# Last sample sequence of a hybrid decoder step: sliding weights turned ahead of the older values, tokens asked for together, first gate tile's tanh ahead of the next tile's splits

## The chip, the cores and the metric

The kernel runs on one core of a Trainium2 chip. A core has TensorE (PE, matrix products and transposes by a product with the identity), VectorE (DVE), ScalarE (ACT), GpSimd (POOL) and SyncE (SP); the last two issue most of the transfers here. Each engine works through its own instructions in order. The metric is the device time of one execution in microseconds, as a median of runs. All of the arithmetic is in 32-bit floats; a factor of a large product is split into a high and a low part, and three of the four partial products are taken.

## What is computed

One layer of a decoder step, on a prompt of 512 tokens and on 8 sample sequences of 8 new tokens with 2048 cached tokens each. Two attention branches (one with forgetting gates, one with compressed, selected and sliding-window keys) go through a projection each, are merged by sigmoid gates, and are followed by an output projection and an MLP. What matters for the change, cut from the reference:

```python
g_fox, g_nsa = jnp.split(jax.nn.sigmoid(mg), 2, axis=-1)     # mg: columns of h @ w_in
...
s = jnp.einsum('btgrd,bwgd->bgrtw', q, kw) * scale - m * dw   # sliding window of a sample sequence
p_w = masked_softmax(s, (dw >= 0) & (dw < WINDOW) & (w_pos >= 0)[None, :])
o_w = jnp.einsum('bgrtw,bwgd->btgrd', p_w, vw)
...
br_fox = jnp.einsum('btk,kd->btd', o_fox.reshape(b, t_len, FOX_QW), lp['w_br_fox'])
br_nsa = jnp.einsum('btk,kd->btd', o_nsa.reshape(b, t_len, NSA_QW), lp['w_br_nsa'])
mix = pm['g_fox'] * br_fox + pm['g_nsa'] * br_nsa
```

The gates need the normalized tokens h of all 576 rows (512 prompt, 64 sample), which earlier in the kernel were written to device memory (`hfd`), turned so that channels lie on the partitions: 8 pieces of 128 channels x 576 tokens.

## The kernel before, in words

The step is a chain of stages: projections, the prompt's attention, the sample sequences' attention (`sample_attention`, L1613, about 430 to 545 us), the mix (`mix_part`, L1967, about 545 to 698 us), the output projection and the MLP.

**The order.** The program is written in one order, and a planner sorts each engine's instructions by its own estimate of when they are ready. Where that isn't wanted the code pins it: `chain` and `link` (L87) string all of PE's instructions one behind another as written, from the sample attention's start to its end and again from the second gate tile on. `issue_after(x)` queues what its block writes on x's engine behind x; instructions of other engines in the block aren't held by it. `dma` (L151) keeps the order of transfers on one queue.

**The sample loop** (L1651). For each of the 8 sequences b: scores (`sequence_scores`, PE, then four reductions on DVE), scores of the new tokens (`new_scores`), the maximum and three exponentials on ACT (`sequence_max`), turns of the weights on PE with copies on ACT (`turn_weights`, into `T` and `TN`), and the products with the values (`values`, into the bank `so`). The sliding window is done for two sequences at a time, n = b // 2: its weights `SWt` are made in the even sequence and turned in the odd one (`window_turned`, L1907: four turns into bank `spw` and one of the new tokens into `spwn`, then two ACT copies to `TW` and `TWn`), then multiplied by the values (`window_values`) and summed by `pair_sums` one pair later. For the last sequence, b = 7, sequence 6's older values (its parts 2 and 3) are written between the scores and `new_scores`, by a function given to `sequence_scores`. The trace names `TW` and `SWt` both `scr`.

**The tokens.** At b = 7 the buffers of sequence 6 are free and become `hL` and `hH`, the low and high parts of h. `tokens_load` (L1602) first writes a few elements of `hL` on ACT from a source that is a gate (so that the loads wait for it) and then asks for the pieces on SP and POOL by turns: pieces 0 to 3 after the new scores, with `CT` as the gate; pieces 4 to 7 in `turn_weights`, with `TN`. Each piece is split: ACT makes `hH`, DVE makes `hL` (L1727 to L1733, four ahead of the last values and four behind). `mix_first` (L1958) takes the products of the high parts for the first gate tile.

**The mix.** For each of 8 tiles of 128 output channels there are two gates (tanh of half the product h w) and two branch products; `branch` multiplies, `closed` adds and splits the sum. Weights come through one ring of three raw buffers (`praw`): a load goes into a buffer, ACT and DVE split it (`stream`, L170), then the buffer is free for the next load. Tile 0 and 1 take their gates as plain products; tiles 2 to 7 take both gates as one 2 x 2 block product with seven multiplications (`pair`, L2079), whose token operands `token_sums` (L2012) makes from the rows of h. For that the rows are loaded again: `rows_ahead` (L2002) writes one element on ACT behind the last high part, and then POOL asks for `hr0` (pieces 0 to 2), `mgtr` (pieces 3 and 7) and `hr1` (pieces 4 to 6). There are four PSUM banks for products (`mmb`); a gate's bank is free when its tanh on ACT has read it, a branch's when DVE has multiplied it.

Of the kernel before, what the change touches and what calls it, by code (L numbers as in the profile page):

```python
# [6 lines left out]
F32 = mybir.dt.float32  # L7
# [3 lines left out]
AF = mybir.ActivationFunctionType  # L11
# [3 lines left out]
P = 128  # L15
D = 1024
NK = D // P
SEQ = 512
NB = 8
NS = 64  # L20
NT = SEQ + NS
HALF = NT // 2
TOK = 2080
# [22 lines left out]
class Step:  # L46
# [1566 lines left out]
    def sample_attention(self, sp, ctx):  # L1613
# [35 lines left out]
        last = NB - 1  # L1649

        for b in range(NB):  # L1651
            n, odd = b // 2, b % 2
            if b and b + 2 < NB:
                self.key_prep(b + 2)
            self.sequence_scores(b, (lambda: self.values(b - 1, range(2, 4))) if b == last else None)
            ahead = not odd and b > 2
            if ahead:
                for o in range(2):
                    self.window_keys(b + o)
            self.new_scores(b)  # L1660
            if not odd:
                self.window_new(n)
            if not odd and b:
                self.values(b - 1, range(1, 4))
            if b == last:
                self.hL = self.keep.tile([P, 5 * D], F32R, tag="r2", bufs=1, name="hL2")[:, 0:NK * NT].rearrange("p (k t) -> p k t", k=NK)
                self.hH = self.rp.tile([P, NK, NT], F32R, tag="rp", name="hH")
                self.tokens_load(range(4), self.CT[0:1, 0:4, None])
            self.sequence_max(b)
            if odd:  # L1670
                self.window_turned(n)
            if b > 1:
                self.sequence_end(b - 2)
                if not odd:
                    self.window_end(n - 1)
            if b < last:
                with self.tc.issue_after(self.last_stat):
                    self.key_turn(b + 1, (0, 1))
            if 0 < b < last and odd:
                self.values(b - 1, range(2, 4))  # L1680
            if b == last - 1:
                self.mix_ahead()
            if odd:
                self.window_values(n)
                if b < last:
                    for o in range(2):
                        self.window_load(b + 1 + o, "gpsimd")
                if b > 1:
                    self.pair_sums(n - 1)
            if b and b + 2 < NB:  # L1690
                self.sample_load(b + 2, range(1 if b % 2 == 0 else 2, 4))
            if b < last:
                with self.tc.issue_after(self.last_stat), self.tc.issue_after(self.last_end) if b > 1 else nullcontext():
                    self.key_counts(b + 1)
                    self.key_turn(b + 1, (2, 3))
            if b == last:
                self.sequence_end(b - 1)
                self.window_end(n)
                ctx.close()
                self.mix_open()  # L1700
                with self.tc.issue_after(self.last_exp):
                    self.w0 = self.gate_weights(0, 0)
            if b == 0:
                for o in range(2):
                    self.window_keys(o)
            if ahead:
                self.window_scores(n)
            self.turn_weights(b)
            if b == 2:
                with self.tc.issue_after(self.last_weights):  # L1710
                    for o in range(2):
                        self.window_keys(b + o)
            if b < last:
                with self.tc.issue_after(self.last_weights):
                    self.last_weights = self.act(self.CT, self.ct).ins
            if b < last:
                self.values(b, range(1 if odd else 2))
            if b + 3 < NB:
                self.sample_load(b + 3, range(1 if odd else 2))
            if not odd:  # L1720
                if not ahead:
                    self.window_scores(n)
                self.window_weights(n)
            if b == 0:
                with self.tc.issue_after(self.last_stat):
                    self.sample_maps(maps)
        with self.tc.issue_after(self.last_weights):  # L1727
            for k in range(4):
                self.split(self.hH[:, k], self.hL[:, k], self.hL[:, k].bitcast(F32))
        self.values(last, range(4))  # L1730
        with self.tc.issue_after(self.last_weights):
            for k in range(4, NK):
# [107 lines left out]
    def turn_weights(self, b):  # L1840

        last = b == NB - 1
        tb = self.trb(f"spn{b}")
        self.tr(tb[:NS, 0:P], self.SN[b % 2])
        self.act(self.TN, tb[:NS, 0:P])
        if last:
            self.tokens_load(range(4, NK), self.TN[0:1, 0:NK - 4, None])
        for i in range(4):
            tb = (self.trb if last and i > 1 else self.mmb)(f"sp{b}{i}")
            for j in range(4):  # L1850
                self.tr(tb[:, P * j:P * j + P], self.S[:, 4 * i + j].rearrange("p q s -> p (q s)"))
            self.last_weights = self.act(self.T[i], tb.rearrange("p (j n) -> p j n", j=4)).ins
# [52 lines left out]
            self.act(self.SWt, self.SWt, AF.Exp, bias=st[:, 2:3], accum_out=st[:, 3:4])  # L1905

    def window_turned(self, i):  # L1907
        tb, tn = self.trb(f"spw{i}"), self.mmb(f"spwn{i}")
        for j in range(4):
            self.tr(tb[:, P * j:P * j + P], self.SWt[:, P * j:P * j + P])  # L1910
        self.tr(tn[:NS, 0:P], self.SWt[:, 512:576])
        self.act(self.TW, tb.rearrange("p (j n) -> p j n", j=4))
        self.act(self.TWn, tn[:NS, 0:P])

    def window_values(self, i):
        col = 256 + 128 * (i % 2)
# [15 lines left out]
        self.mctx = ExitStack()  # L1932
        self.pqr = self.pool("pqr", self.mctx, side="right")

    def gate_weights(self, e, x):
        return self.stream(self.pqr, self.cols(self.I["w_in"], TOK + D * x + P * e, P), [P, NK, P], "wm", f"{x}_{e}", raws=0, parts=1)

    def mix_ahead(self):

# [27 lines left out]
    def mix_part(self, pq, pr, mix2):  # L1967
# [16 lines left out]
            return pq.tile([P, 2, 2, HALF], F32, tag="c", bufs=2, name=f"mgt{e}")  # L1984

        def gate(out, pb):
            self.act(out, pb, AF.Tanh, scale=0.5)

        def branch(e, x, w, C):
            pbs = [half(f"br{e}{x}", w, (hs(oH, 4 * x), hs(oL, 4 * x)), 4, hf) for hf in range(2)]  # L1990
# [4 lines left out]
        def br_weights(e, x):  # L1995
            return self.stream(pq, self.br_src(x, e), [P, 4, P], "wb", f"{x}_{e}", raws=0, parts=1)
# [3 lines left out]
            self.split_pack(mix2[:, e], C[:, 0].rearrange("p g t -> p (g t)"))  # L2000

        def rows_ahead(C):  # L2002
            R = [self.pw0.tile([P, 4, 512], F32, tag="w0", bufs=2, name=f"hr{j}").rearrange("p a c -> p (a c)")[:, 0:3 * NT]
                 .rearrange("p (k t) -> p k t", k=3) for j in range(2)]
            R3 = C.rearrange("p f g t -> p (f g t)").rearrange("p (j k t) -> p j k t", j=2, k=1)
            with self.tc.issue_after(self.last_weights):
                self.act(R[0][0:1, 0, 0:1], hH[0:1, NK - 1, 0:1].bitcast(F32))
            for r, k in ((R[0], slice(0, 3)), (R3[:, :, 0], slice(3, 8, 4)), (R[1], slice(4, 7))):
                self.dma("gpsimd", r, self.hfd[:, k])
            return [(slice(0, 3), R), (slice(3, 4), [R3[:, j] for j in range(2)])]  # L2010

        def token_sums(rows):  # L2012
            t12 = self.keep.tile([P, 5 * D], F32R, tag="r1", bufs=1, name="mt12")[:, 0:16 * HALF].rearrange(
                "p (a k t) -> p a k t", a=4, k=4)
            t4 = pq.tile([P, 2, 4, HALF], F32R, name="mt4")
            T = [(t12[:, 0], t12[:, 1]), (t12[:, 2], t12[:, 3]), (b[0][1][0], b[0][1][1]), (t4[:, 0], t4[:, 1])]
            cut = [slice(0, HALF), slice(HALF, NT)]
            for ks, R in rows:
                (r11, r12), (r21, r22) = [[r[:, :, c] for c in cut] for r in R]

                def keep(t, x):
                    self.split(t[0][:, ks], t[1][:, ks], x)

                self.tt(r11, r12, r11, sub)
                keep(T[0], r11)
                self.tt(r12, r22, r12, sub)
                self.tt(r22, r22, r11, sub)
                keep(T[1], r22)
                self.tt(r21, r21, r22, sub)
                keep(T[3], r21)  # L2030

            def last():
                for ks, R in rows:
                    self.split(T[2][0][:, ks], T[2][1][:, ks], R[0][:, :, cut[1]])

            return T, last
# [83 lines left out]
        for x in range(2):  # L2120
# [8 lines left out]
                            self.mm(p, w[:, k, :], h(k, hf), k == 0 and c == 0, k == NK - 1 and c == 2)  # L2129
            for hf in range(2):  # L2130
                gate(C[:, x, hf], pbs[hf][:, 0:HALF])
        for x in range(2):
            branch(0, x, ws[x][1], C)
        closed(0, C)

        ws = [(self.gate_weights(1, x), br_weights(1, x)) for x in range(2)]
        T, last = token_sums(rows)
        C = cs(1)
        self.chain = ""
        for hf in (1, 0):  # L2140
# [566 lines left out]
```

## Time and profile before

| what | value |
|---|---|
| median of 3 runs | 1157.57 us (1155.44 to 1160.59) |
| the profiled execution's own time | 1160.21 us |
| its span | 1158.5 us |
| busy PE, DVE, ACT, POOL | 1093.5, 822.5, 544.4, 243.1 us |
| PE's share of the chain that ended last | 74% |
| moved by the transfers | 191.75 MB, mean 166 GB/s |

A line of the groups or of the order of time has a line number of the code (often that of a helper: L77 is every product, L83 every turn, L112 every ACT operation, L131 the low half of every split, L155 a transfer), the engine, the operation, and output<-inputs by the program's names without numbers. In the order of time the first number is the start in the span and the second the time it covers; `x4` says that four are merged, and a bracket gives the idle time of the engine before it and what ended it. SPq is SP's queue of transfers. PE is pipelined, so its instructions overlap.

### The profile page before, as it was taken

To read this page: it belongs to the slowest core of one execution; us is meant where nothing else is said; L and a number is where in the kernel's file an instruction comes from. 1 tells how busy PE (TensorE), PEld (TensorE's weight loads), DVE (VectorE), ACT (ScalarE), POOL (GpSimd) and SP (SyncE) were. 2 spreads that over 40 slices of the span, in tenths; PEclk is the share of its full clock that TensorE was granted. 3 is DMA by queue.
4 is the path that set the end of the run, shared out by engine and by line. 5 is a ranking of instruction groups with operands and counts; after the bars stand their busy time and mean duration, and the time that the engine had idled before them with its cause. 6 is when DMAs were issued, how large, how long until landed. Compare 5 with 4: busy or idle time off the path is not lost.

```text
span 1158.5 us, 24596 instructions
## 1 busy us (share of the span) xinstructions
PE 1093.5 (94%) x9089; PEld 941.1 (81%) x9089; DVE 822.5 (71%) x2011; ACT 544.4 (47%) x1146; POOL 243.1 (21%) x341
## 2 busy tenths in 40 slices
PE   3999999989999997887999999999999999999998
PEld 3887799989666654556999999998989989898896
DVE  5898666685787857776878667759757567475668
ACT  3466643444777754456545434473424324143230
POOL 7541000001211536440000000013222122221202
PEclk9999999999999998998999999999999999999999
DMA  8998584764786589995632454152313224132232
GB/s 202 296 268 219 200 267 148 254 204 134 248 272 202 146 264 356 361 329 138 183 86 79 110 178 140 47 174 90 110 37 109 73 74 130 52 110 62 66 119 82
DMA packets 167513, 191.75 MB, mean 166 GB/s; under 512 B 17849, under 2 KB 145282, under 8 KB 165218
## 3 DMA queue, kind: packets, MB, share of 16 engines
q1 hardware_dynamic: 151650, 146.80, 42.8%
q0 software_dynamic: 13568, 42.34, 11.2%
q8 instruction: 71, 1.16, 0.4%
q10 hardware_dynamic: 2176, 1.05, 0.4%
q14 instruction: 48, 0.39, 0.1%
HBM read 179.89 MB, written 31.16 MB: 182 GB/s over the span
## 4 chain that ended last, share of the span: by engine, by line
PE 74%; DVE 9%; DMA 7%; ACT 4%; issue 3%; POOL 1%; SPq 1%; POOLq 1%; DVEq 0%; ACTq 0%
PE dn L77 18%; PE hid L77 6%; PE z L77 5%; PE wo L77 4%; PE up L77 4%; PE upx L77 3%; PE upv L77 3%; PE br L77 3%; PE ss L77 3%; DMA winr<-in_w_in 3%; PE upy L77 2%; PE upz L77 2%; PE upu L77 2%; PE mgv L77 2%; PE ada L77 1%
## 5 line engine op out<-in xcount | busy, mean ns | idle before, releaser
L100 DVE TENSOR_TENSOR acc<-acc,dn 128x512 f32<-128x512 f32 x66 | 44.5, 685 | 55.4 <-PE dn L77 55.4
L77 PE MATMUL hid<-xh,w1hlk 128*128 128x256 f32 (+1 forms) x192 | 47.4, 340 | 16.5 <-ACT xh L112 16.5
L77 PE MATMUL z<-winh,h2r 128*128 128x264 f32 (+1 forms) x288 | 57.7, 290 | 4.0 <-ACT adw L112 4.0
L77 PE MATMUL z<-winh,h 128*128 128x264 f32 (+1 forms) x288 | 56.8, 287 | 0.0
L112 ACT ACTIVATE xh<-cpg 128x512 fp32r<-128x512 f32 x64 | 37.6, 623 | 36.3 <-PE hid L77 22.5
L112 ACT ACTIVATE u<-c 128x512 fp32r<-128x512 f32 x64 | 24.1, 434 | 58.9 <-PE dn L77 45.1
L77 PE MATMUL hid<-xh,w1hlv 128*128 128x256 f32 (+1 forms) x192 | 47.9, 341 | 4.0 <-ACT w1hlv L112 2.5
L2374 POOL TENSOR_TENSOR wur<-wur 128x512 f32<-128x512 f32 x12 | 19.9, 1658 | 150.3 <-DVE wu1l L131 54.9
L131 DVE TENSOR_TENSOR xl<-cpg,xh 128x512 fp32r<-128x512 f32 x64 | 42.4, 683 | 11.5 <-ACT xh L112 11.5
L77 PEld LDWEIGHTS z<-winh,h2r 128*128 128x128 f32 x288 | 45.8, 190 | 5.3 <-ACT adw L112 4.2
L77 PEld LDWEIGHTS hid<-xh,w1hlk 128*128 128x128 f32 x192 | 33.1, 201 | 20.4 <-ACT xh L112 16.7
L77 PEld LDWEIGHTS z<-winh,h 128*128 128x128 f32 x288 | 46.6, 193 | 0.0
L77 PE MATMUL z<-winl,h 128*128 128x264 f32 (+1 forms) x160 | 44.9, 287 | 0.5 <-DVE winl L131 0.5
L77 PE MATMUL z<-winl,h2r 128*128 128x264 f32 (+1 forms) x160 | 44.7, 286 | 0.0
L470 DVE STREAM_TRANSPOSE cpg<-cpg 128x1024 f32<-128x1024 f32 (+1 forms) x36 | 39.1, 1108 | 6.9 <-DMA cpg<-in_cache_nsa_kv 6.9
L155 POOL DMA_DIRECT2D cpg<-in_cache_nsa_kv x72 | 37.9, 527 | 28.4 <-issue 13.2
L155 POOL DMA_DIRECT2D sr<-in_cache_nsa_kv x64 | 34.6, 542 | 35.1 <-DMA fr<-foxD 10.1
L77 PE MATMUL br<-oH,wbh 128*128 128x288 f32 x128 | 38.4, 300 | 2.6 <-ACT mgt L112 2.6
L77 PEld LDWEIGHTS hid<-xh,w1hlv 128*128 128x128 f32 x192 | 33.6, 202 | 8.2 <-ACT w1hlv L112 2.7
L77 PE MATMUL br<-oL,wbh 128*128 128x288 f32 x128 | 38.4, 300 | 0.0
L77 PE MATMUL br<-oH,wbl 128*128 128x288 f32 x128 | 38.4, 300 | 0.0
L1805 DVE CUSTOM_DVE_ANT_1 sS<-ss,scr 128x512 f32<-128x512 f32 x32 | 20.2, 687 | 22.1 <-PE ss L77 22.1
(887 smaller groups left out, 3628.4 us busy)
## 6 DMA issues: line engine op xcount, KB each, us to landing
adw<-in_w_ada SPq DMA_DIRECT2D x16, 1024.0 KB
foxD<-in_cache_fox_kv SPq DMA_DIRECT2D x128, 128.0 KB
wur<-in_w_up SPq DMA_DIRECT2D x32, 512.0 KB
wdr<-in_w_down SPq DMA_DIRECT2D x32, 512.0 KB
wada<-in_w_ada SPq DMA_DIRECT2D x8, 1024.0 KB
sr<-in_cache_nsa_kv SPq DMA_DIRECT2D x64, 128.0 KB
fr<-foxD SPq DMA_DIRECT2D x16, 512.0 KB
fr<-foxD POOLq DMA_DIRECT2D x16, 512.0 KB, 7.9
```

What stands on the lines that cost most here:

```text
L77: ins = self.nc.tensor.matmul(out, a, b, start=start, stop=stop, skip_group_check=True)
L100: self.nc.vector.tensor_tensor(out, a, b, op=op)
L112: return self.nc.scalar.activation(out, in_, f, **kw)
L131: self.splits.append((eng or self.nc.vector).tensor_tensor(l, x, h.bitcast(F32), op=OP.subtract).ins)
L155: self.issued[eng] = getattr(self.nc, eng).dma_start(out, in_).ins
L470: self.flipped = self.nc.vector.transpose(v, v).ins
L1805: self.nc.vector.tensor_tensor_reduce(self.S[:, :, q, :], pbs[q].rearrange("p (c s) -> p c s", s=32), self.ramp[:, None, 32 * (q % 2):32 * ...
L2374: gp(a12, a12, a11, op=OP.subtract)
```

## The change

In the last sequence, `window_turned` (the four turns into `spw` and the copy to `TW`) is written ahead of sequence 6's older values, directly behind the scores. The turn of the new tokens into `spwn` and the copy to `TWn` become `window_turned_new`, written ahead of the exponentials. For the other odd sequences both follow each other where they were, and the `TW` copy stands ahead of the `spwn` turn. The loads of the token pieces 4 to 7 take `TWn` as their gate in place of `TN`. The two larger row loads (`hr0`, `hr1`) are asked for behind the fourth high part; the third (`mgtr`) stays in `rows_ahead`, now with no gate of its own. The ACT halves of the splits of the second tile's gate weights, and of the token sums up to the last two, are queued behind the first tile's last tanh.

```diff
-            self.sequence_scores(b, (lambda: self.values(b - 1, range(2, 4))) if b == last else None)
+            self.sequence_scores(b, self.last_between if b == last else None)
...
+            if b == last:
+                self.window_turned_new(n)
             self.sequence_max(b)
-            if odd:
+            if odd and b < last:
                 self.window_turned(n)
+                self.window_turned_new(n)
...
+        self.rows_again = [self.pw0.tile([P, 4, 512], F32, tag="w0", bufs=2, name=f"hr{j}").rearrange("p a c -> p (a c)")
+                           [:, 0:3 * NT].rearrange("p (k t) -> p k t", k=3) for j in range(2)]
+        with self.tc.issue_after(self.last_high):
+            self.last_weights = self.act(self.rows_again[0][0:1, 0, 0:1], self.hH[0:1, 3, 0:1].bitcast(F32)).ins
+        for j in range(2):
+            self.dma("gpsimd", self.rows_again[j], self.hfd[:, 4 * j:4 * j + 3])
         self.values(last, range(4))
...
-        if last:
-            self.tokens_load(range(4, NK), self.TN[0:1, 0:NK - 4, None])
...
     def window_turned(self, i):
-        tb, tn = self.trb(f"spw{i}"), self.mmb(f"spwn{i}")
+        tb = self.trb(f"spw{i}")
         for j in range(4):
             self.tr(tb[:, P * j:P * j + P], self.SWt[:, P * j:P * j + P])
+        self.act(self.TW, tb.rearrange("p (j n) -> p j n", j=4))
+
+    def window_turned_new(self, i):
+        tn = self.mmb(f"spwn{i}")
         self.tr(tn[:NS, 0:P], self.SWt[:, 512:576])
-        self.act(self.TW, tb.rearrange("p (j n) -> p j n", j=4))
         self.act(self.TWn, tn[:NS, 0:P])
+        if i == NB // 2 - 1:
+            self.tokens_load(range(4, NK), self.TWn[0:1, 0:NK - 4, None])
+
+    def last_between(self):
+        self.window_turned(NB // 2 - 1)
+        self.values(NB - 2, range(2, 4))
...
-    def gate_weights(self, e, x):
-        return self.stream(self.pqr, self.cols(self.I["w_in"], TOK + D * x + P * e, P), [P, NK, P], "wm", f"{x}_{e}", raws=0, parts=1)
+    def gate_weights(self, e, x, first=None):
+        return self.stream(self.pqr, self.cols(self.I["w_in"], TOK + D * x + P * e, P), [P, NK, P], "wm", f"{x}_{e}", raws=0, parts=1,
+                           pin=first and (first,))
...
-            self.act(out, pb, AF.Tanh, scale=0.5)
+            self.last_gate = self.act(out, pb, AF.Tanh, scale=0.5).ins
...
-            for r, k in ((R[0], slice(0, 3)), (R3[:, :, 0], slice(3, 8, 4)), (R[1], slice(4, 7))):
-                self.dma("gpsimd", r, self.hfd[:, k])
+            self.dma("gpsimd", R3[:, :, 0], self.hfd[:, 3:8:4])
...
                 def keep(t, x):
-                    self.split(t[0][:, ks], t[1][:, ks], x)
+                    with self.tc.issue_after(first):
+                        self.split(t[0][:, ks], t[1][:, ks], x)
...
+        first = self.last_gate
         for x in range(2):
             branch(0, x, ws[x][1], C)
         closed(0, C)
 
-        ws = [(self.gate_weights(1, x), br_weights(1, x)) for x in range(2)]
-        T, last = token_sums(rows)
+        ws = [(self.gate_weights(1, x, first), br_weights(1, x)) for x in range(2)]
+        T, last = token_sums(rows, first)
```

More of the change, by code (lines that the diff above doesn't have):

```diff
@@ L2002, in rows_ahead, with token_sums @@
         def rows_ahead(C):
-            R = [self.pw0.tile([P, 4, 512], F32, tag="w0", bufs=2, name=f"hr{j}").rearrange("p a c -> p (a c)")[:, 0:3 * NT]
-                 .rearrange("p (k t) -> p k t", k=3) for j in range(2)]
+            R = self.rows_again
             R3 = C.rearrange("p f g t -> p (f g t)").rearrange("p (j k t) -> p j k t", j=2, k=1)
-            with self.tc.issue_after(self.last_weights):
-                self.act(R[0][0:1, 0, 0:1], hH[0:1, NK - 1, 0:1].bitcast(F32))
-            for r, k in ((R[0], slice(0, 3)), (R3[:, :, 0], slice(3, 8, 4)), (R[1], slice(4, 7))):
-                self.dma("gpsimd", r, self.hfd[:, k])
+            self.dma("gpsimd", R3[:, :, 0], self.hfd[:, 3:8:4])
             return [(slice(0, 3), R), (slice(3, 4), [R3[:, j] for j in range(2)])]
-        def token_sums(rows):
+        def token_sums(rows, first):
             t12 = self.keep.tile([P, 5 * D], F32R, tag="r1", bufs=1, name="mt12")[:, 0:16 * HALF].rearrange(
```

## The prediction

> **What bounds the kernel now.** I read the page first. It says that TensorE carries most of the chain that ended last, so I asked where TensorE does not run densely near the edits. That is the view of the stages.
>
> ```profile
> span 1158.5 us, 24596 instructions
> ...
> 601.30:700.00 98.70, 98.53 (x742) 98.02 (x741) 69.72 (x131) 41.54 (x73) 2.64 (x5) 1.00 0.45 128
> 700.00:766.00 66.00, 65.04 (x541) 64.40 (x541) 44.71 (x139) 30.94 (x63) 2.77 (x5) 1.00 0.35 110
> 766.00:1158.50 392.50, 387.54 (x2236) 345.93 (x2234) 267.47 (x401) 136.82 (x253) 88.97 (x60) 1.00 0.29 88
> ```
>
> Columns: stretch, length, then busy time of PE, PE's weight loads, DVE, ACT and POOL, the granted clock, DMA share, GB/s. From 601.3 us on PE is busy for nearly all of each stretch, at full clock. A start earlier there by some microseconds therefore moves the end by as much. What decides is when PE reaches 601.3, so next I read the chain of waits from the last sample sequence to there (start, length, what).
>
> ```profile
> 534.10 2.26 ACT sS L112 x4
> 536.36 0.49 ACT scr L112
> ...
> 536.89 1.82 PE so L77 x48
> 538.72 1.05 PE accS L77 x16
> 539.77 0.35 PE spn L83
> ...
> 541.01 0.61 ACT spT L112
> ...
> 542.24 6.11 DMA hL<-hfd
> ...
> 549.77 0.75 DVE hL L131
> ...
> 551.19 1.14 DVE wml L131
> ...
> 552.34 11.04 DMA wmr<-in_w_in
> ...
> 570.38 1.22 DVE wml L131
> ...
> 572.23 7.15 DMA wgr<-in_w_in
> ...
> 589.31 6.70 DMA wgr<-in_w_in
> ...
> 599.44 1.85 PE mgv L77 x12
> ```
>
> Two things run through it. Up to 541 it is a queue: the copy of the turned sliding weights (`scr`, 536.36) stands behind the last sequence's exponentials on ACT, and PE's sliding values, sums and turns stand behind that copy. From 551 on it is the ring of three raw weight buffers: a split frees a buffer (551.19), the next load takes 11.04 us, and so on to `mgv` at 599.44. PE itself shows two gaps, in the order of time of its instructions and ACT's (the bracket is the idle time and what ended it):
>
> ```profile
> 528.71 0.19 ACT L112 ACTIVATION_READ_ACCUMULATOR scr<-scr,swst 128x1 f32 x1
> 531.76 0.66 PE L83 MATMUL spw<-identF,scr 128*128 128x128 f32 x4
> 532.25 0.27 PE L83 MATMUL spwn<-identF,scr 128*64 128x128 f32 x1
> 545.16 0.40 PE L77 MATMUL mg<-hH,wmh 128*128 128x288 f32 x1
> 558.70 0.29 PE L77 MATMUL mg<-hL,wmh 128*128 128x288 f32 x1
> 563.41 1.06 ACT L112 ACTIVATE wmh<-wmr 128x1024 fp32r<-128x1024 f32 x1 [6.51 <-DMA wmr<-in_w_in]
> 564.37 0.69 ACT L112 ACTIVATE mgt<-mg 128x288 f32<-128x288 f32 x2
> 564.82 0.40 PE L77 MATMUL br<-oH,wbh 128*128 128x288 f32 x1 [2.65 <-ACT mgt L112]
> 569.53 0.39 PE L77 MATMUL mg<-hH,wmh 128*128 128x288 f32 x1
> ```
>
> The first gap goes from 532.52 (end of `spwn`) to 536.89, 4.37 us. The second is the 2.65 us before 564.82: a tanh (`mgt`) waits on ACT behind a split (`wmh`) whose weights are still on the way. The granted clock (last but two) fell around both:
>
> ```profile
> 537.00:538.00 1.00, 1.00 (x36) 0.83 (x40) 0.00 (x0) 0.00 (x1) 0.00 (x0) 0.50 0.00 0
> 542.00:543.00 1.00, 1.00 (x11) 0.83 (x9) 0.00 (x0) 0.81 (x2) 0.03 (x1) 0.79 1.01 106
> 566.00:570.00 4.00, 4.00 (x21) 4.00 (x20) 4.00 (x7) 1.96 (x4) 0.00 (x0) 0.57 0.22 66
> ```
>
> **The change part by part.**
>
> *Sliding weights turned ahead of the older values.* No operation is added; four turns (0.66) go ahead of sequence 6's late values on PE, and the copies to TW and TWn go ahead of the exponentials on ACT. Their input is there at 528.9, before PE ends the scores. PE's order then ends at the same 532.5, with `TW` copied under the values. The sliding values start there: 1.82 and 1.05 us lead to 535.4, and `spn` (0.35) to 535.8. The exponentials end at 536.36; they wait for DVE, not for this. The first turned weights can be copied from about 536.5. One operation moves up against them: the high half of the first gate weights, 1.06 us by the `wmh` row, allowed once the last exponential is issued, and ahead in program order. I take it in front (537.5); the other bound is behind (536.5). The four copies cost 2.02 where the clock was full, against 2.74 here (541.01 to 543.75):
>
> ```profile
> 523.37 2.02 ACT L112 ACTIVATE spT<-sp 128x512 f32<-128x512 f32 x4
> 542.66 1.09 ACT L112 ACTIVATE spT<-sp 128x512 f32<-128x512 f32 x2 [0.19 <-PE sp L83]
> ```
>
> So they end at 539.6 (or 538.6) in place of 543.75: **4.2 us earlier** (bound 5.2). The first matrix product of the mix moves from 545.16 to about 541.0.
>
> *Tokens asked for together.* Four more loads are issued near 533 in place of 541, two on SP's queue and two on POOL's; nothing due there waits behind them, since SP's next issue needs a buffer that is freed only after the first weights' split. Eight pieces of 288 KB are 2.36 MB:
>
> ```profile
> hr<-hfd POOLq DMA_DIRECT2D x2, 864.0 KB, 7.1
> hL<-hfd POOLq DMA_DIRECT2D x4, 288.0 KB, 4.4
> 542.00:548.00 6.00, 6.00 (x176) 5.49 (x174) 3.65 (x7) 5.10 (x9) 0.03 (x1) 0.96 0.89 242
> 543.63 2.98 ACT L112 ACTIVATE hH<-hL 128x576 fp32r<-128x576 f32 x5
> 544.35 2.77 DVE L131 TENSOR_TENSOR hL<-hL,hH 128x576 fp32r<-128x576 f32 x4 [3.24 <-ACT hH L112]
> 550.44 0.75 DVE L115 COPY oT<-accS 128x256 f32<-128x256 f32 x2
> ```
>
> At the 242 GB/s of that stretch they need 9.8 us from 532.2, so they are in at 542, when ACT, after four splits from 539.6 (2.98 for five, 0.6 each), asks for the fifth. I book nothing for it; at the rows' bounds it is 1 us of wait or of gain. The cover is the four splits themselves. DVE's eight low halves (0.69 each by the row) then set the pace and end near 546, 4.5 earlier than 550.52.
>
> *Rows asked for earlier.* Two row loads (864 KB each) move from behind the eighth high half to behind the fourth, by a one-element ACT copy; the third follows without a gate. They no longer start together with the load of 552.34, which in the trace took 11.04 us where an equal load later took 6.70 and 7.15. With the splits 4.7 earlier that load is issued at 547.6, and lands between 554.3 (6.70) and 558.6 (11.04). I take 554.3 to 555, since most of the rows' bytes are then through.
>
> *Tanh ahead of the splits.* The next tile's weight split and the row splits on ACT are queued behind the first tile's last tanh. PE no longer stands 2.65 us, and without the gap the clock isn't cut: the stretch of 566 to 570 ran at 0.57, so 4 x 0.43 = **1.7 us** were lost. What is queued behind the tanh now is the split `wmh`; its product waits for it. The first tile's products end at 559.0 (558.70 and 0.29), so now at 554.8; tanh (0.69) to 555.5; `wmh` to 556.6, `wml` (1.23 in DVE's order) to 557.8. Before it was 565.7 (563.41, 1.06, then 1.22): **7.9 us earlier**.
>
> The Trainium skill, TensorE: Matmul & The Clock Gate, Part 1, puts the drop to half rate at an idle window of about 3.4 us. Here 2.65 us of idle were enough (the 0.57 above), so the trace is followed; by the rule alone the 1.7 would not be tied to this gap, and PE's part of the sum would be that much less.
>
> **The sum.** Two chains meet at 599.44. PE's own: 4.2 + 2.65 + 1.7 = 8.55 us earlier at the next tile's first product (569.53). The ring's: 7.9 earlier, kept through its later loads of 7.15 and 6.70, which follow from splits that move with it. The later one counts: 7.9. The profiled execution took 1160.21 (span 1158.5), so 1152.3; the median shown, 1157.57, lies 2.64 below it, so **1149.7**.
>
> **The rivals.**
>
> A, the ring's load stays at 11.04 us although the rows go earlier (the tokens, now together, and the rows still crowd it). Then the split ends 4.8 earlier, not 7.9, PE waits for it or for the banks behind DVE, and the time is 1152.8. For it: the stretch is full of loads. Against: rows and load no longer start within 1.5 us.
>
> B, the first edit doesn't do what it says: the order that the program's planner writes leaves TW's copy behind the exponentials. Then 2.65 + 1.7 = 4.35 on PE, about 4 on the ring: 1153.5. Against it: ACT is idle from 528.9 on but for one small copy.
>
> C, the clock. With the values gone ahead, the stretch before the last values is mostly turns. The trace speaks against a cut: an equal run of turns in sequence 6 had full clock.
>
> ```profile
> 522.23 2.22 PE L83 MATMUL sp<-identF,sS 128*128 128x128 f32 x16
> 525.00:526.00 1.00, 0.48 (x36) 0.32 (x24) 1.00 (x3) 0.91 (x2) 0.00 (x0) 1.00 1.17 211
> ```
>
> If it is cut as after the second gap, 1.7 of PE's 8.55 go back, 6.85 remain, 1150.7. The Trainium skill, the same page, Part 4, says that transposes do not count as busy for the gate; the row of sequence 6 does not show such a cut.
>
> D, the other side: DVE takes the row differences, no longer held by late data in the plan, ahead of the second gate tile's `wml` (551.19 before), and stands in order until both row loads are in. If these take the 11.04 us of the crowded load from 544, they land at 555; two differences of 1.05, the copies of the sums (0.75) and `wml` follow to 559.1, against 552.33. PE then stands 6.7 us more, and pays 1.7 for the clock, less the 4.35 of the tanh: 4 us slower, 1161.6. It decides from a landing after about 551. Against it: in the trace DVE took the first row difference only among the late splits.
>
> E, more than forecast: the weights' half goes behind the copies, the loads are quick, and the wait of 1.0 us at `mgv` is gone too. About 10 us, 1147.6.
>
> **How the numbers follow.** Forecast 0.48, A 0.22, B 0.10, C 0.05, D 0.07, E 0.08. The likeliest gives 1149.7. The range: below, E and the distance from median to lowest run shown (2.1) give about 1145.8; above, A and B with the spread of runs give 1156.8, and D is left out. All but D lie on one side. A change under 0.5% (5.8 us) can't be told from none here. Faster by more than that: 0.9 of the forecast, C and E mostly, a third of A, a little of B: 0.64. Within: the rest of A and B and what is left of the forecast, 0.30. Slower: most of D, 0.06.
>
> **What would show it.** Right: `TW` copied before the exponentials; PE's gap near 533 under 1 us and the clock at 1.00 through 543; the mix's first product near 541; no bracket before the second branch's products and no cut near 567; the gate weights' load after 547 at some 7 us; `mgv` near 591.5. Wrong: a load of 11 us there (A), the copy behind the exponentials (B), a cut clock near 540 (C), DVE idle on a row load near 547 (D). The sum falls also if PE, once earlier, meets a new wait after 601.

## The result, and the profile after

Nine runs of the changed kernel gave a median of 1150.67 us (1145.09 to 1153.18), nine of the kernel before 1158.13 (1155.44 to 1162.27): a ratio of 0.9917 with a 95% interval of 0.9894 to 0.9941. The forecast was 1149.7. The profiled execution took 1150.76 us (span 1149.1), against 1160.21 (1158.5).

The chain of waits of the changed kernel over the same stretch (start, length, what):

```profile
536.09 0.95 ACT wmh L112
537.03 0.17 ACT TN L112
537.20 0.04 issue
537.25 0.66 PE sp L83 x4
...
539.49 1.01 PE so L77 x48
540.50 2.36 PE mg L77 x16
...
543.47 10.76 PE mg L77 x80
554.24 6.36 PE br L77 x48
560.59 12.70 PE mg L77 x96
...
579.73 6.64 DMA wgr<-in_w_in
...
589.80 1.85 PE mgv L77 x12
```

Before, this stretch held four transfers: a token piece (6.11 us), the load of 11.04 us and two more loads of weights. Now PE's products run one behind the other from 540.5 to 574, and one load is left in the chain, ahead of `mgv`. The same in the order of time, of all engines that the change touches:

```profile
530.62 0.60 ACT L112 ACTIVATE scr<-spw 128x512 f32<-128x512 f32 x1 [2.02 <-PE spw L83]
532.70 0.21 ACT L112 ACTIVATE hL<-TWn 1x4 fp32r<-1x4 f32 x1
532.97 0.65 PE L77 MATMUL so<-wr,scr 128*32 128x64 f32 x32 [0.61 <-DVE ss L1829]
534.66 0.30 PE L83 MATMUL spn<-identF,sN 128*64 128x128 f32 x1
540.43 0.40 PE L77 MATMUL mg<-hH,wmh 128*128 128x288 f32 x1
541.94 1.13 POOL L155 DMA_DIRECT2D hr<-hfd  x2 [7.62 <-DMA wbr<-in_w_br_nsa]
547.23 0.39 SPq L182 DMA_DIRECT2D wmr<-in_w_in  x1
553.87 0.81 ACT L112 ACTIVATE mgt<-mg 128x288 f32<-128x288 f32 x2 [2.76 <-PE mg L77]
554.72 1.06 ACT L112 ACTIVATE wmh<-wmr 128x1024 fp32r<-128x1024 f32 x1
589.80 0.53 PE L77 MATMUL mgv<-hH,wms 128*128 128x288 f32 x2 [0.54 <-DVE mgt L2116]
```

`TW` (here `scr`) is copied at 530.62 in place of 536.27, ahead of the exponentials; PE takes the sliding values from 532.97 in place of 536.89. The row loads are issued at 541.94 in place of 550.97. The gate weights' load is issued at 547.23, and at 554.72 its split starts with no bracket, so it took 7.5 us at most, not 11.04. Of PE's two gaps the first is down from 4.37 to 0.61 us and the second is gone. The granted clock (last but two) is full where it was cut:

```profile
537.00:538.00 1.00, 0.76 (x16) 0.59 (x20) 0.94 (x1) 1.00 (x4) 0.00 (x0) 1.00 1.03 404
566.00:570.00 4.00, 4.00 (x33) 4.00 (x32) 4.00 (x8) 1.21 (x3) 0.00 (x0) 1.00 0.80 197
601.30:700.00 98.70, 98.53 (x749) 97.75 (x747) 71.99 (x131) 42.45 (x71) 2.67 (x5) 1.00 0.45 132
```

From 601 on PE is as dense as before.

**One measure for all kernels.** Executions of one kernel differ by several microseconds, and the traces show where: the last sequence is reached early or late. The start of its last score products lay anywhere from 522.33 to 533.84 us in the fourteen profiles here, though the edits hardly touch the work ahead of it (in the other odd sequences the `TW` copy is written ahead of the `spwn` turn, but in the profiles ACT and PE take them in the same order as before). So the profiles are compared from that row on, to three others: the first gate product of the mix, the first gate product of the second tile (what stood at 569.53 before), and the first of the products called `mgv<-hH` (599.44 before). For before and after the first row is

```profile
529.79 0.50 PE L77 MATMUL ss<-CT,W 32*128 32x512 f32 x4 [0.39 <-issue]
```

```profile
529.50 0.50 PE L77 MATMUL ss<-CT,W 32*128 32x512 f32 x4 [0.40 <-issue]
```

(before, then after). One execution stands behind each row of steps. The table gives the three steps, their sum and what is left to the end of the span, in us, each a difference of two starts in one profile; then the median of all runs and the ratio to the runs of the kernel before on the same chip. "Without" is the changed kernel less a part, "alone" the kernel before with a part.

| kernel | to first gate | to tile 2 | to `mgv` | sum | rest | median | ratio (95%) |
|---|---|---|---|---|---|---|---|
| before | 15.37 | 24.37 | 29.91 | 69.65 | 559.06 | 1158.13 | |
| changed | 10.93 | 20.00 | 29.37 | 60.30 | 559.30 | 1150.67 | 0.9917 (0.9894 to 0.9941) |
| changed, again | 11.19 | 20.00 | 28.74 | 59.93 | 559.06 | 1146.57 | 0.9905 (0.9874 to 0.9937) |
| without pins | 10.64 | 20.18 | 28.67 | 59.49 | 558.81 | 1148.13 | 0.9906 (0.9870 to 0.9943) |
| without pins, again | 10.91 | 20.08 | 28.68 | 59.67 | 558.92 | 1148.52 | 0.9915 (0.9884 to 0.9946) |
| without the token sums' pin | 10.65 | 20.13 | 29.14 | 59.92 | 558.94 | 1148.81 | 0.9914 (0.9883 to 0.9945) |
| without tokens together | 10.71 | 21.42 | 28.90 | 61.03 | 558.59 | 1147.86 | 0.9903 (0.9867 to 0.9939) |
| without early rows | 10.91 | 21.68 | 31.39 | 63.98 | 558.77 | 1150.16 | 0.9930 (0.9903 to 0.9956) |
| without sliding turns | 15.15 | 20.02 | 28.67 | 63.84 | 558.93 | 1151.20 | 0.9938 (0.9914 to 0.9963) |
| pins alone | 15.40 | 20.91 | 33.61 | 69.92 | 560.77 | 1154.84 | 0.9974 (0.9960 to 0.9989) |
| pins alone, again | 14.87 | 22.07 | 31.56 | 68.50 | 560.55 | 1156.72 | 0.9977 (0.9955 to 0.9999) |
| early rows alone | 14.96 | 20.66 | 28.81 | 64.43 | 559.12 | 1152.32 | 0.9959 (0.9939 to 0.9978) |
| sliding turns alone | 10.72 | 24.51 | 29.56 | 64.79 | 559.21 | 1153.28 | 0.9968 (0.9948 to 0.9989) |
| sliding turns and early rows | 10.72 | 20.29 | 28.73 | 59.74 | 558.66 | 1148.01 | 0.9895 (0.9866 to 0.9923) |

The change took 9.35 us out of the sum. Which part took what is the matter of the experiments.

### The profile page after: what moved, and what is told of

It reads as the page before. It is cut to its first block, busy times and chain, and to the rows that moved or that the text cites. A ratio compares the mean times of both kernels' runs of the same rounds, so it can differ in the third digit from the quotient of the medians.

```text
span 1149.1 us, 24598 instructions
## 1 busy us (share of the span) xinstructions
PE 1090.6 (95%) x9089; PEld 938.0 (82%) x9089; DVE 822.3 (72%) x2011; ACT 544.6 (47%) x1146; POOL 240.4 (21%) x341
## 4 chain that ended last, share of the span: by engine, by line
PE 78%; DVE 8%; DMA 6%; ACT 4%; SPq 2%; issue 2%; DVEq 0%; ACTq 0%
PE dn L77 18%; PE hid L77 5%; PE z L77 5%; PE br L77 4%; PE wo L77 4%; PE up L77 4%; PE upx L77 3%; PE upv L77 3%; PE ss L77 3%; PE mg L77 2%; SPq L155 2%; DMA winr<-in_w_in 2%; PE upy L77 2%; PE upz L77 2%; PE upu L77 2%
```

## The experiments

**Without the pins.** The splits are no longer queued behind the tanh.

```diff
-        ws = [(self.gate_weights(1, x, first), br_weights(1, x)) for x in range(2)]
+        ws = [(self.gate_weights(1, x), br_weights(1, x)) for x in range(2)]
...
-                    with self.tc.issue_after(first):
-                        self.split(t[0][:, ks], t[1][:, ks], x)
+                    self.split(t[0][:, ks], t[1][:, ks], x)
```

> The changed kernel without the two pins behind the first tile's last tanh; all else kept. ACT then has the second tile's weight split ahead of that tanh again. Theory (two chains: the pins matter only while the load is late): with the rows asked early the load is in at about 554.7, the split ends near 555.7 and the tanh near 556.4, before PE asks for the bank at 557.2; so no gap and no cut clock, and the time is that of the changed kernel within 1 us (1150.7 to 1151.7). Rival (each part is worth what it was booked at): the gap of 2.65 us and the 1.7 us of cut clock come back, about 4.35 us more, 1155.

ACT does have the split ahead of the tanh again. SP's queue and ACT in the order of time:

```profile
550.44 0.39 SPq L182 DMA_DIRECT2D wmr<-in_w_in  x1
557.67 1.06 ACT L112 ACTIVATE wmh<-wmr 128x1024 fp32r<-128x1024 f32 x1 [3.34 <-DMA wmr<-in_w_in]
558.64 0.70 ACT L112 ACTIVATE mgt<-mg 128x288 f32<-128x288 f32 x2
```

The load takes 7.2 us, the tanh ends at 559.34, and PE has no gap there: the step to the second tile is 20.18 against 20.00. The sum is 59.49. The time, 1148.13, is far from the rival's 1155. So the pins are not needed in the changed kernel: the early rows bring the load in sooner, and with it split and tanh. Repeated beside the changed kernel:

> The changed kernel once more, beside the next two on one chip. From the last sequence's last score products to the seventh product of the third gate tile: 60.3 us as in its first profile, give or take 0.5.

> The changed kernel without the pins behind the tanh, once more. Theory now (the pins give nothing once the rows go early, and make DVE free the raw buffers a little later): 59.5 us over the same stretch, and a time some 1 us under the changed kernel, which may be too little to tell. Rival (the 2.5 us by which its first median lay lower were chance of the chips): the same time or more.

59.93 with the pins, 59.67 without; the medians are 1146.57 and 1148.52, their intervals overlap almost wholly. The lower median of the first time did not repeat, and no kernel here is shown to beat the changed one.

```diff
-                    with self.tc.issue_after(first):
-                        self.split(t[0][:, ks], t[1][:, ks], x)
+                    self.split(t[0][:, ks], t[1][:, ks], x)
```

> The changed kernel with the pin on the weights' splits kept and the pin on the token sums' splits taken away. If the token sums' pin is what delays DVE's release of the raw buffers, 59.5 us over that stretch; if it is the weights' pin, 60.3 as in the changed kernel.

59.92: between the two, and all five profiles lie within about 0.8 us. What difference the pins make to the release of the raw buffers is too small to be told.

**The pins alone**, on the kernel before.

> The kernel before with the two pins alone (tanh ahead of the next tile's splits); sliding turns, tokens and rows as before. Theory (two chains): PE loses its gap of 2.65 us at 562 and runs at full clock to the end of the branch products near 565, but the second tile's weights still land at 563.4 and their low part at 565.7, and the ring to mgv at 599.4 is as before: gain of 0 to 1.5 us, 1156.6 to 1158.1. Rival (parts add up): 4.35 us gained, 1153.8.

> The kernel before with the two pins alone, once more: its runs lay 3 us below those of before, while its profile showed 69.9 us over the stretch from the last sequence's last score products to the seventh product of the third gate tile, against 69.65 before. Theory (the ring alone sets that stretch, the pins give nothing): 69.5 to 70 us again, and a time within 2 us of before. Rival (the profile caught a late load, the pins do give something): 67 us or less, and 3 us gained.

As in the changed kernel, PE no longer stands at the first tile's branch products. But it stands later. PE's brackets in the first of the two profiles, then the clock:

```profile
567.02 0.37 PE L77 MATMUL mg<-hH,wmh 128*128 128x288 f32 x1 [0.77 <-DVE mgt L109]
571.10 0.40 PE L77 MATMUL mg<-hH,wml 128*128 128x288 f32 x1 [0.57 <-DVE wml L131]
...
600.63 0.54 PE L77 MATMUL mgv<-hH,wms 128*128 128x288 f32 x2 [2.87 <-DVE mgt L2113]
```

```profile
600.00:602.00 2.00, 1.37 (x8) 1.37 (x9) 2.00 (x5) 1.04 (x2) 0.00 (x0) 0.86 0.00 0
602.00:604.00 2.00, 2.00 (x11) 2.00 (x10) 2.00 (x5) 1.21 (x2) 0.00 (x0) 0.50 0.00 0
```

The step to the second tile is 3.46 shorter, that to `mgv` 3.70 longer: the gap of 2.65 came back as several further on, the longest of 2.87 at `mgv` (0.99 before), cut clock and all, since the load still took 10.89 us and the ring was no faster. The second profile shows the same waits, somewhat shorter (68.50 in all, with 1.85 us at `mgv`). The timed runs show a gain of 0.2 to 0.3%, some 3 us, which the profiles do not (rest included, 630.69 and 629.05 against 628.71). Whether and where those 3 us lie stays open. The two profiled executions took 1163.07 and 1160.09 us, the slowest of 13 and the second slowest of 12, so they may not stand for the rest. The runs decide neither for the theory nor against the rival: the rival's 4.35 us (a ratio of 0.9962) lie inside both intervals, near their lower ends, and 1154.84 lies nearer to its 1153.8 than to the theory's 1156.6 to 1158.1.

**The early rows**, taken away and alone. Taken away:

```diff
-        with self.tc.issue_after(self.last_high):
-            self.last_weights = self.act(self.rows_again[0][0:1, 0, 0:1], self.hH[0:1, 3, 0:1].bitcast(F32)).ins
-        for j in range(2):
-            self.dma("gpsimd", self.rows_again[j], self.hfd[:, 4 * j:4 * j + 3])
...
-            self.dma("gpsimd", R3[:, :, 0], self.hfd[:, 3:8:4])
+            with self.tc.issue_after(self.last_weights):
+                self.act(R[0][0:1, 0, 0:1], hH[0:1, NK - 1, 0:1].bitcast(F32))
+            for r, k in ((R[0], slice(0, 3)), (R3[:, :, 0], slice(3, 8, 4)), (R[1], slice(4, 7))):
+                self.dma("gpsimd", r, self.hfd[:, k])
```

> The changed kernel with the three row loads asked for behind the eighth high part again, as before; sliding turns, tokens together and pins kept. Theory: the gate weights' load, issued near 547, starts together with the rows again and takes about 11 us in place of 7; its low part is ready 3 to 4 us later, PE stands before the second tile's products, and the time is 3 us above the changed kernel (1153.5, rival A of the prediction made on purpose). Rival: the load's length has nothing to do with the rows, or DVE's order hides it: no change, 1150.7.

> The kernel before with the two larger row loads asked for behind the fourth high part, alone. Theory: the gate weights' load of 552.3 is less crowded (some 8 us in place of 11), so the split and the tanh behind it come 2 to 3 us earlier and most of PE's gap at 562 goes: gain of 2 to 3 us, 1155 to 1156. Rival (the load's time is its own, or the rows now crowd the late token pieces, which land at 548.4): no gain, or 1 to 2 us lost, 1158 to 1160.

The load of the second tile's first gate weights, by the chain of waits, where the rows were issued within 2.2 us of it: without early rows, and with the sliding turns alone,

```profile
542.78 12.01 DMA wmr<-in_w_in
```

```profile
545.66 11.03 DMA wmr<-in_w_in
```

and, by the order of time, issue and split with the early rows alone:

```profile
547.41 0.38 SPq L182 DMA_DIRECT2D wmr<-in_w_in  x1
554.14 1.06 ACT L112 ACTIVATE wmh<-wmr 128x1024 fp32r<-128x1024 f32 x1 [2.28 <-DMA wmr<-in_w_in]
555.10 0.70 ACT L112 ACTIVATE mgt<-mg 128x288 f32<-128x288 f32 x2
```

6.7 us. So the same load takes 10.9 to 12.0 us in the five profiles where it starts with the rows, and 6.7 to at most 7.6 in the nine where the two larger row loads went 5.3 to 6.5 us ahead. Alone the early rows shorten the sum by 5.2 (64.43), all but 0.4 of it behind the first gate product. That is more than the 2 to 3 expected, since the cut clock and the wait at `mgv` go as well; the timed runs agree (1152.32, a ratio of 0.9959). Taken away they cost 3.7 of the sum (63.98): PE stands at the second tile, in spite of the pins, and for 1.64 us at `mgv`.

```profile
557.64 0.37 PE L77 MATMUL mg<-hH,wmh 128*128 128x288 f32 x1 [1.51 <-DVE mgt L109]
561.73 0.40 PE L77 MATMUL mg<-hH,wml 128*128 128x288 f32 x1 [0.54 <-DVE wml L131]
```

The timed runs show less of that loss. The median of 1150.16 us is not the 1153.5 forecast but nearly the rival's 1150.7, and the interval of its ratio overlaps the changed kernel's. Against two kernels timed with it on the same chip that keep the early rows, the ones without the pins (1148.13) and without tokens together (1147.86), it is some 2 us slower. The loss in the sum is thus shown by one profile, and its size in the whole time is not.

**The sliding turns**, taken away and alone. Taken away:

```diff
-            self.sequence_scores(b, self.last_between if b == last else None)
+            self.sequence_scores(b, (lambda: self.values(b - 1, range(2, 4))) if b == last else None)
...
-            if b == last:
-                self.window_turned_new(n)
             self.sequence_max(b)
-            if odd and b < last:
+            if odd:
```

> The changed kernel with the sliding weights of the last pair turned and copied behind the exponentials again (values of the older sequence first); tokens 4 to 7 keep TWn as gate, so they too are asked for some 4 us later. Theory: PE's gap of 4.4 us and the cut clock near 537 return, the first gate product goes back from 540.4 to about 545, and the time is 4.2 to 5 us above the changed kernel: 1155 to 1156. Rival (the ring alone sets the end and has slack from the early rows): under 2 us, 1152.

> The kernel before with the sliding turns of the last pair ahead of the older values, alone (tokens behind TN, rows and tanh as before). Theory: everything from the first gate product on moves by 4 to 5 us, with the load of 11 us, the gap at the tanh and the cut clock behind it kept: gain of 4 to 5 us, 1153 to 1154. Rival: the ring does not move with it, gain under 2 us, 1156.5.

Without them PE's first gap and the cut clock are back, in PE's order of time and the stages:

```profile
529.45 1.08 PE L77 MATMUL so<-wr,scr 128*32 128x64 f32 x32 [4.37 <-ACT scr L112]
```

```profile
530.00:532.00 2.00, 2.00 (x50) 1.49 (x44) 0.26 (x2) 1.06 (x1) 1.06 (x2) 0.50 0.56 136
532.00:534.00 2.00, 2.00 (x16) 1.88 (x14) 1.66 (x4) 0.70 (x2) 0.00 (x0) 0.50 1.02 380
534.00:536.00 2.00, 2.00 (x58) 1.83 (x60) 0.00 (x0) 1.74 (x5) 0.00 (x0) 0.87 0.55 180
```

The first gate product comes 4.2 later (15.15 against 10.93), and 3.5 are left of it at `mgv`. The median, 1151.20 us, is some 3 us above the same two kernels on that chip, but below the 1155 to 1156 forecast, and nearer to the rival's 1152. Alone they bring it 4.65 sooner (10.72) and the sum down by 4.9 (64.79), with the gap at the tanh kept, 2.42 us, and the clock cut behind it; the median of 1153.28 is as forecast:

```profile
558.12 0.40 PE L77 MATMUL br<-oH,wbh 128*128 128x288 f32 x1 [2.42 <-ACT mgt L112]
```

**Tokens together**, taken away: pieces 4 to 7 wait for `TN` again.

```diff
-        if i == NB // 2 - 1:
-            self.tokens_load(range(4, NK), self.TWn[0:1, 0:NK - 4, None])
...
         self.act(self.TN, tb[:NS, 0:P])
+        if last:
+            self.tokens_load(range(4, NK), self.TN[0:1, 0:NK - 4, None])
```

> The changed kernel with pieces 4 to 7 of the tokens asked for behind TN again (about 537.2 in place of 533). Theory: they are in near 543.5, 2 us after ACT wants the fifth at 541.5; 1 to 2 us of wait, 1151.7 to 1152.7. Rival 1: the cover of the four splits holds, no change, 1150.7. Rival 2: the tokens are what the gain hangs on, 4 us more, 1154.7.

The first gate product is where it was (10.71); the sum is 61.03, 0.7 to 1.1 more. This profile does show a wait of the kind expected: the last token piece came late, and PE stood for its split.

```profile
543.60 0.40 PE L77 MATMUL mg<-hH,wmh 128*128 128x288 f32 x1 [0.87 <-ACT hH L112]
```

But in the next kernel the tokens wait for `TN` too, PE has no such gap, and the sum is as low as any. The timed runs (1147.86) show no loss. So asking early was worth about 1 us in one of these two profiles and nothing in the other.

**The two parts that carry it**, without pins and without tokens together.

> The kernel before with the sliding turns and the early rows alone, without pins and with the tokens behind TN. Theory (these two carry the gain and add up): 69.65 - 4.9 - 5.2 = 59.6 us over the same stretch, and the time of the changed kernel, 1147 to 1149. Rival (tokens together or pins are needed as well): 61 us or more, 1150 to 1152.

59.74, as forecast by adding (59.6), and a ratio of 0.9895 (0.9866 to 0.9923): the whole gain, from two of the four parts. Its `mgv` has no bracket:

```profile
587.84 0.43 PE L77 MATMUL mgv<-hH,wms 128*128 128x288 f32 x2
```

## Why the prediction was right, and where it was not

**The time** was 1149.7, measured 1150.67; within the range, and faster as said. Against the profiled execution the sum was 7.9 us off 1160.21, and the profile shows 9.4 (of the span), 0.3 of it ahead of the change. The medians differ by 7.5; that this is nearer to 7.9 than the 9.4 is partly chance, since single executions of one kernel differ by more than that.

**Sliding turns: right.** Booked at 4.2 on the first gate product; 4.44 in the changed kernel, 4.65 alone. The weights' half did go ahead of the turned weights (`wmh` at 536.09, then `TN`), as taken.

**Tokens: right at nothing.** Without them the sum grew by at most 1.1 us, in one profile of two.

**Rows: the value was right, the weight was not.** The load was taken to land 7 us behind its issue; it took 7.5 at most here, and 6.7 to 7.4 in the profiles where a bracket of the split gives it. But the row loads appear in the sum only as what shortens the ring's chain. They are worth 5.2 by themselves.

**Tanh ahead of the splits: this step failed as it was credited.** The prediction said that the pins take away the 2.65 us and the 1.7 of cut clock. Both did go, but they go without the pins as well. The tanh was late because the split ahead of it waited for a late load; once the load is in 4 us sooner, split and tanh are through before PE asks for the bank, in whatever order. With the late load the pins, by the profiles, only carry the gap down the ring to `mgv` (2.87 us); the timed runs leave them up to some 3 us, and that stays open. The sum came out well all the same: PE's chain was credited to the wrong part but had the right size, since the early rows take away the same gap. At the second tile's first product PE was 8.81 us earlier (39.74 less 30.93 in the table), forecast 8.55. The 1.7 in it were read off one execution; the last section shows that a gap of one length is not always followed by a cut. Asked for the parts one by one, the prediction would have taken 4.35 from PE's chain without the pins, where nothing is lost beside the early rows.

**The ring: mis-sized by 1.7.** Expected `mgv` at 591.5, measured 589.80. The forecast took the ring as the later of the two chains. It was hardly that: PE waited 0.54 us for it at `mgv` in this profile, and not at all in the second one of the same kernel. The low part of the first split ended at 558.54, near the 557.8 forecast; behind it DVE took the second gate's low part at once (558.82), so that the loads after it were issued from 560.07, where the forecast, by a plain shift of 572.23, had 564.3.

**The rivals.** A (the load stays at 11 us) is what the kernel without early rows shows: 12.01 us there, and 3.7 lost in the profile, where the rival had 3.1 (in the timed runs some 2). B (`TW` stays behind the exponentials) is the kernel without sliding turns; the planner did as written. C (turns let the clock fall): in the changed kernel PE did nothing but turn from 534.66 to 537.9, with one wait of 0.45 us, at full clock (1.00 in each microsecond from 534 to 538). The rule of the Trainium skill behind it, TensorE: Matmul & The Clock Gate, Part 4, that transposes don't count as busy in the same way, is not seen here in a stretch of 3.2 us. D (DVE stands on the rows) did not come: the first row difference was taken at 548.33, behind the second gate's low part. Of E, the wait at `mgv` halved to 0.54 in one profile and was gone in others.

## What to carry to other kernels

An engine's wait behind another's queue (a tanh behind a split) may only be the last link of a late transfer; ask first why the transfer was late. Changing the order of the queue then, in the profiles here, moves the wait along, while starting the transfers that crowd it at another time removes it. And where executions differ ahead of the change, compare profiles from a row that all kernels share up to one behind the change: two profiles of one kernel agreed there within 0.4, 0.2 and 1.4 us, so that differences above 1.5 us can be told, where the medians of whole runs leave 3.

## What the runs showed of the hardware

The granted clock of TensorE fell to half after shorter gaps than the rule that the prediction cited from the Trainium skill (TensorE: Matmul & The Clock Gate, Part 1: an idle window of about 3.4 us): after 2.42 us with the sliding turns alone and 2.87 with the pins alone, as after the 2.65 before. After 1.51 us without the early rows, and after 1.85 in the second profile of the pins alone, the outcomes differ: in the first case the clock stayed at 1.00, in the second it was cut too.

```profile
558.00:560.00 2.00, 2.00 (x18) 2.00 (x17) 2.00 (x4) 2.00 (x4) 0.00 (x0) 1.00 0.44 129
```

```profile
598.00:600.00 2.00, 2.00 (x13) 2.00 (x14) 2.00 (x5) 0.56 (x2) 0.00 (x0) 0.75 0.00 0
600.00:602.00 2.00, 2.00 (x10) 2.00 (x10) 2.00 (x4) 1.33 (x3) 0.00 (x0) 0.50 0.00 0
```

(The first row is without the early rows, behind its gap at 557.64; the other two are the pins alone, again, behind the gap that ended at 597.85.) But the length of the gap alone does not decide. Some 81 us ahead of the last score products PE waits for cached keys, in the kernel before and in the changed one alike. The wait was 2.84 us before, and the clock was cut behind it; it was 2.83 us in the changed kernel, and the clock stayed at 1.00 in each microsecond from 446 to 455:

```profile
448.83 0.66 PE L77 MATMUL ss<-sr,scr 32*32 32x512 f32 x8 [2.84 <-DMA sr<-in_cache_nsa_kv]
451.00:452.00 1.00, 1.00 (x12) 0.29 (x4) 0.00 (x0) 0.00 (x0) 0.54 (x1) 0.50 1.00 353
```

```profile
448.21 0.66 PE L77 MATMUL ss<-sr,scr 32*32 32x512 f32 x8 [2.83 <-DVE sr L1795]
451.00:452.00 1.00, 1.00 (x17) 0.66 (x17) 1.00 (x3) 0.26 (x1) 0.87 (x2) 1.00 1.05 378
```

(Before, then after.) So gaps of 1.85 to 2.87 us can be enough in this kernel, and a cut cannot be foretold from the length of one gap. What else decides was not tried.

Not expected either was how far the time of one kernel moves ahead of all edits: 11.5 us between the earliest and the latest start of the last score products over fourteen profiles, while the rest behind `mgv` agreed within 2.2 us. What makes the earlier stages so uneven wasn't tried.
